# Tying each background sum of a two-layer mixer to the VectorE instruction traced before it

## Chip, cores and metric

One Trainium2 chip, one core of it. The metric is device time in microseconds of one execution of the whole kernel; the profile is one such execution on the same core.

## The reference

The network has two layers, each with one mixer. A mixer normalises 256 latent and 256 context tokens of width 2048, applies a scale and a shift, and projects them with `w_in`. Two attention groups work on the projections (8 heads of grouped-query attention with rotary positions, 8 heads of latent attention), their outputs are gated by a SiLU and projected back by `w_out`, and the result is added to the stream with a gate per channel:

```python
for l in range(DEPTH):
    shift, scale, gate = jnp.split(sc @ w_ada[l] + b_ada[l], 3, axis=-1)
    ...
    h_lat = rms_norm(x, norm_g[l]) * (1.0 + scale[:, None]) + shift[:, None]
    ...
    x = x + gate[:, None] * merge_groups(o_a, lat_a[3], o_b, lat_b[3], w_out[l])
```

What matters here is the first line: `shift`, `scale` and `gate` are matrix-vector products, for two vectors (`c` and `c_ctx`), of 2048 inputs with 6144 outputs in each layer. Everything is float32.

## The kernel before

**The main work.** Each weight matrix is streamed from HBM in tiles of 512 KB. `wtile` (line 107) loads a tile on SP's DMA queue into `raw` (4 buffers), rounds it on ScalarE into `hi` (line 116, 3 buffers) and subtracts it in two halves into `lo` (line 118, 2 buffers). The subtraction runs on VectorE, and on GpSimd (POOL) for every fifth tile. `mm3` (lines 143 to 145) multiplies each pair of tiles three times on TensorE: high by high, low by high, high by low. A tile is reused for 512 tokens in layer 0 and for 256 in most of layer 1. Attention is in `softmax` (lines 605 to 616), `mix` (628, 636) and `attend`; the last VectorE instruction of a head group is the product of line 636 with the gate.

**The background work.** The first layer's shift and scale are made on TensorE at the start. The rest (the first layer's gate, the second layer's scale, shift and gate) is made on VectorE while TensorE multiplies. `ada_rest` (line 308) is a generator that goes through 128 steps. A step (in `ada_half`, line 263) loads 128 rows of the transposed `w_adaT`, 1024 columns at a time, into `rad` (512 KB, 3 buffers), and forms the dot products of these rows with the broadcast vector `cb`: one multiply-and-sum (line 286) for each half row and each of the two vectors, so four VectorE sums a step, and two a step for the second layer's gate, which needs one vector. All sums write their unneeded elementwise product to `junk`, of which there is one buffer. `ada_done` (line 291) adds the two column halves; for scale and shift it writes `mod` (line 208), which the second layer's normalisation reads, and for a gate it transposes the row on TensorE (line 303), copies it (305), stores it to DRAM (306), and `out_steps` loads it again (line 794, `gt`) for the product of line 823 (`go`).

**What sets the order.** The program is traced in one order, and the order of each engine's queue is set from it when the kernel is built, by a modelled timeline (`TCKW`) in which an instruction is queued when its inputs and buffers are there and its priority, its place in the trace, is the best of those that wait. The sums are given a priority 1500 places further back (`BG_LATER`), so they go where nothing else is ready on VectorE. `wtile` traces background steps right after its `lo` instructions, at `bg_rate` steps a tile (1.3, 1.1, 0.5 in layer 0 and 0.4 in layer 1); what is left is traced by `bg_flush` in layer 1, after the first pair of latent heads. `rad` loads are queued on SP behind the last `raw` load (`raw`, line 93), and all loads share SP's queue, in order.

Of the kernel before, what the change touches and what calls it, by code (L numbers as in the profile page):

```python
# [13 lines left out]
ALU = mybir.AluOpType  # L14
# [36 lines left out]
class Net:  # L51
# [211 lines left out]
    def ada_half(self, half, work):  # L263


        nc = self.nc
        hs = slice(half * 1024, half * 1024 + 1024)
        if half not in self.cb:
            self.cb[half] = self.cb_tile()
            with self.behind():  # L270
                nc.sync.dma_start(out=self.cb[half], in_=self.sc_d[:, hs].partition_broadcast(P))
        cb = self.cb[half]
        for l, kind, vs in work:
            if (l, kind) not in self.sums:
                self.sums[l, kind] = [self.cp.tile([P, KT, len(vs)], F32, name=self.nm("as"), tag=f"as{kind}{h}") for h in range(2)]
            out = self.sums[l, kind][half]
            r0 = (0 if l == 0 else D + kind * D)
            for k in range(KT):
                r = self.raw(self.a["w_adaT"][r0 + k * P : r0 + (k + 1) * P, hs], 1, 1024, "rad")[1][:, 0, :]
                for v in vs:  # L280
                    o = out[:, k, v : v + 1]
                    for i in range(NG):
                        cs = slice(i * 1024 // NG, (i + 1) * 1024 // NG)
                        junk = self.tp.tile([P, 1024 // NG], BF16, tag="junk", name=self.nm("junk"), bufs=1)
                        with self.tc.high_priority(offset=-BG_LATER):
                            nc.vector.tensor_tensor_reduce(  # L286
                                out=junk, in0=r[:, cs], in1=cb[:, v, cs], scale=1.0, scalar=o if i else 0.0, op0=ALU.mult, op1=ALU.add, accum_out=o
                            )
                yield

# [924 lines left out]
```

## Time and profile before

| | us |
|---|---|
| median of 3 runs (1394.38 to 1397.32) | 1396.55 |
| the profiled execution | 1398.29 |
| its span, first to last instruction | 1396.5 |
| TensorE (PE) busy | 1328.5 |
| VectorE (DVE) busy | 1078.8 |
| ScalarE (ACT) busy | 580.6 |
| GpSimd (POOL) busy | 404.2 |

The profiled execution lies 1.8 us around its span (what comes before the first and after the last instruction) and 1.7 us above the median. Busy times are sums over the whole span; the stages below have different limits. An engine's instruction shows with its start, its length and, in brackets, how long the engine stood idle before it and what ended that idle time.

### The profile page before, as it was taken

The numbers are of one execution on the slowest core, as the hardware profiler recorded it, in microseconds if no ns is written. First come the engines' busy times: TensorE is split into PE (matmuls) and PEld (weight loads), VectorE is DVE, ScalarE is ACT, GpSimd is POOL, SyncE is SP. The second block draws the span as 40 slices with busy tenths as digits, with TensorE's granted clock in tenths as the row PEclk, the third lists the DMA queues.
The fourth block names the chain that finished last, engine by engine and source line by source line (L and its number), as shares of the span: only waits on it lengthen the run. The fifth ranks groups of instructions, "written<-read, shape, count | busy, mean of one in ns | idle before, by whom it ended". The sixth has DMA issues, their size and how long they took to land.

```text
span 1396.5 us, 21018 instructions
## 1 busy us (share of the span) xinstructions
PE 1328.5 (95%) x7516; PEld 1126.5 (81%) x7516; DVE 1078.8 (77%) x2297; ACT 580.6 (42%) x961; POOL 404.2 (29%) x385
## 2 busy tenths in 40 slices
PE   5999998997999999999999999999999999999996
PEld 5776677786887998788887888889898889888884
DVE  3776589999998999999985536966788676766566
ACT  4322213434351332454532224654554544454543
POOL 0110014533230422222222214433344231323235
PEclk9999999998999999999999999999999999999998
DMA  9997854554635676544465446565866657634444
GB/s 306 331 316 267 307 166 136 166 165 145 185 125 197 217 241 199 167 136 143 170 222 183 149 131 201 175 193 161 268 219 191 195 152 249 234 108 127 159 142 144
DMA packets 141128, 268.31 MB, mean 192 GB/s; under 512 B 8304, under 2 KB 53856, under 8 KB 139616
## 3 DMA queue, kind: packets, MB, share of 16 engines
q1 hardware_dynamic: 141024, 266.97, 59.2%
q8 instruction: 59, 0.97, 0.3%
q14 instruction: 45, 0.37, 0.1%
HBM read 260.61 MB, written 6.33 MB: 191 GB/s over the span
## 4 chain that ended last, share of the span: by engine, by line
PE 50%; DVE 15%; DMA 7%; issue 4%; ACT 3%; POOL 2%; SPq 0%; DVEq 0%; POOLq 0%; ACTq 0%
PE acc L145 14%; PE acc L144 14%; PE acc L143 14%; DVE junk L286 5%; DMA rad<-in_w_adaT 5%; DVE lo L118 4%; PE att L605 3%; DMA raw<-in_w_in 2%; PE att L628 2%; DVE sm L610 1%; PE att L145 1%; PE att L143 1%; PE att L144 1%; DVE y L150 1%; ACT hi L116 1%
## 5 line engine op out<-in xcount | busy, mean ns | idle before, releaser
L116 ACT CAST hi<-raw 128x1024 fp32r<-128x1024 f32 (+2 forms) x279 | 272.0, 977 | 409.4 <-PE acc L144 235.9
L118 DVE TENSOR_TENSOR lo<-raw,hi 128x512 fp32r<-128x512 f32 (+2 forms) x446 | 307.0, 730 | 105.0 <-PE acc L145 47.5
L118 POOL TENSOR_TENSOR lo<-raw,hi 128x512 fp32r<-128x512 f32 (+2 forms) x112 | 153.9, 1395 | 460.5 <-PE acc L145 290.1
L143 PE MATMUL acc<-hi,h 128*128 128x512 f32 (+1 forms) x672 | 239.2, 360 | 7.5 <-DVE g L466 3.8
L144 PE MATMUL acc<-hi,h 128*128 128x512 f32 (+1 forms) x672 | 238.9, 358 | 0.0
L145 PE MATMUL acc<-lo,h 128*128 128x512 f32 (+1 forms) x672 | 227.8, 361 | 6.5 <-DVE lo L118 5.2
L286 DVE CUSTOM_DVE_ANT_0 junk<-rad,cb 128x512 bf16<-128x512 f32 x224 | 167.8, 749 | 67.3 <-DMA rad<-in_w_adaT 65.0
L286 DVE CUSTOM_DVE_ANT_0 junk<-rad,cb,as 128x512 bf16<-128x512 f32 x224 | 190.7, 851 | 3.4
L144 PE MATMUL acc<-h,lo 128*128 128x512 f32 (+1 forms) x512 | 171.0, 340 | 2.7 <-DVE lo L118 2.7
L145 PE MATMUL acc<-h,hi 128*128 128x512 f32 (+1 forms) x512 | 169.9, 338 | 0.0
L616 POOL TENSOR_SCALAR p<-p,sm 128x512 f32<-128x512 f32 (+1 forms) x96 | 86.6, 908 | 277.1 <-DVE sm L614 245.2
L143 PE MATMUL acc<-h,hi 128*128 128x512 f32 (+1 forms) x512 | 163.9, 341 | 1.5 <-DVE g L470 1.2
L143 PEld LDWEIGHTS acc<-hi,h 128*128 128x128 f32 x672 | 127.0, 189 | 30.4 <-issue 8.7
L144 PE MATMUL acc<-hi,y 128*128 128x512 f32 x384 | 149.4, 391 | 0.6 <-DVE y L150 0.6
L143 PE MATMUL acc<-hi,y 128*128 128x512 f32 x384 | 148.8, 393 | 0.8 <-ACT y L149 0.8
L145 PEld LDWEIGHTS acc<-lo,h 128*128 128x128 f32 x672 | 125.1, 190 | 27.6 <-DVE lo L118 8.2
L145 PE MATMUL acc<-lo,y 128*128 128x512 f32 x384 | 143.0, 394 | 2.5 <-DVE lo L118 1.4
L144 PEld LDWEIGHTS acc<-hi,h 128*128 128x128 f32 x672 | 127.3, 190 | 16.1
L144 PEld LDWEIGHTS acc<-h,lo 128*128 128x128 f32 x512 | 96.6, 189 | 13.4 <-DVE lo L118 4.0
L143 PEld LDWEIGHTS acc<-h,hi 128*128 128x128 f32 x512 | 93.4, 189 | 14.2 <-issue 2.5
L145 PEld LDWEIGHTS acc<-h,hi 128*128 128x128 f32 x512 | 96.6, 189 | 9.8
L145 PEld LDWEIGHTS acc<-lo,y 128*128 128x128 f32 x384 | 71.9, 188 | 19.6 <-DVE lo L118 4.2
(218 smaller groups left out, 2254.0 us busy)
## 6 DMA issues: line engine op xcount, KB each, us to landing
rad<-in_w_adaT SPq DMA_DIRECT2D x128, 512.0 KB, 4.6
raw<-in_w_in SPq DMA_DIRECT2D x125, 512.0 KB, 4.4
raw<-in_w_out SPq DMA_DIRECT2D x72, 512.0 KB, 4.1
ra<-in_w_ada SPq DMA_DIRECT2D x32, 1024.0 KB, 9.1
raw<-in_w_in SPq DMA_DIRECT2D x48, 288.0 KB, 3.1
raw<-in_w_ukv SPq DMA_DIRECT2D x16, 512.0 KB, 3.4
raw<-in_w_uq SPq DMA_DIRECT2D x12, 512.0 KB, 3.8
xT<-in_xT SPq DMA_DIRECT2D x8, 512.0 KB, 8.1
```

Of the source, the lines that this page charges most:

```text
L116: nc.scalar.copy(h, t)
L118: e.tensor_tensor(out=lo[:, c], in0=t[:, c], in1=fr(h[:, c]), op=ALU.subtract)
L143: mm(out, lhsT=ah, rhs=bh, start=first, stop=False)
L144: mm(out, lhsT=al, rhs=bh, start=False, stop=False)
L145: return mm(out, lhsT=ah, rhs=bl, start=False, stop=last)
L150: self.nc.vector.tensor_tensor(out=lo, in0=src, in1=fr(hi), op=ALU.subtract)
L286: nc.vector.tensor_tensor_reduce(out=junk, in0=r[:, cs], in1=cb[:, v, cs], scale=1.0, scalar=o if i else 0.0, op0=ALU.mult, op1=ALU.add, a ...
L605: self.order = nc.tensor.matmul(banks[j], lhsT=q[:, qs], rhs=k[:, ks], start=i == 0, stop=i == len(score) - 1)
L610: nc.vector.tensor_reduce(out=nb[:, c], in_=v, axis=AX.X, op=ALU.max)
L616: nc.gpsimd.tensor_scalar(out=pr[j], in0=pr[j], scalar1=l[:, j : j + 1], scalar2=1.0, op0=ALU.mult, op1=ALU.mult)
L628: nc.tensor.transpose(b[:, k, j * P : (j + 1) * P], pr[j][:, (i + k) * P : (i + k + 1) * P], self.ident)
```

## The change

The call that makes a sum is wrapped in one that queues the instruction behind the VectorE instruction traced just before it. It is an order on VectorE's queue alone: the sum may come any distance behind that instruction, and no longer ahead of it. For the first sum of a step the instruction before it is in most cases the second half of the `lo` of the tile that `wtile` has just made; where that `lo` is on POOL, it is whatever VectorE instruction was traced last; within a step it is the sum before.

```diff
                         with self.tc.high_priority(offset=-BG_LATER):
-                            nc.vector.tensor_tensor_reduce(
-                                out=junk, in0=r[:, cs], in1=cb[:, v, cs], scale=1.0, scalar=o if i else 0.0, op0=ALU.mult, op1=ALU.add, accum_out=o
+                            self.tc.keep_in_program_order(
+                                nc.vector.tensor_tensor_reduce(
+                                    out=junk, in0=r[:, cs], in1=cb[:, v, cs], scale=1.0, scalar=o if i else 0.0, op0=ALU.mult, op1=ALU.add, accum_out=o
+                                )
                             )
```

## Rows read from the trace of the kernel before

**Rows 1.** The page's head and busy times: us, share of the span, instructions.

```profile
span 1396.5 us, 21018 instructions
...
PE 1328.5 (95%) x7516; PEld 1126.5 (81%) x7516; DVE 1078.8 (77%) x2297; ACT 580.6 (42%) x961; POOL 404.2 (29%) x385
```

**Rows 2.** Stages: window, length, PE, PEld, DVE, ACT, POOL busy, PEclk, DMA, GB/s.

```profile
174.00:245.00 71.00, 66.44 (x286) 53.77 (x285) 65.39 (x140) 18.40 (x27) 22.14 (x22) 0.98 0.47 149
...
316.00:339.00 23.00, 15.36 (x76) 13.32 (x76) 20.74 (x58) 8.76 (x21) 10.02 (x14) 0.70 0.41 129
...
424.00:476.00 52.00, 47.28 (x255) 40.54 (x254) 44.81 (x104) 12.82 (x25) 16.89 (x16) 0.97 0.58 199
476.00:700.00 224.00, 219.12 (x1299) 193.53 (x1298) 218.00 (x537) 97.70 (x182) 52.77 (x54) 1.00 0.55 178
700.00:772.00 72.00, 71.18 (x345) 58.99 (x344) 50.25 (x117) 23.48 (x40) 17.47 (x15) 1.00 0.57 197
772.00:840.00 68.00, 68.00 (x302) 56.31 (x301) 26.71 (x48) 19.07 (x28) 17.15 (x13) 1.00 0.48 151
...
840.00:868.00 28.00, 28.00 (x127) 23.15 (x126) 17.63 (x22) 12.82 (x17) 12.19 (x12) 1.00 0.65 215
...
985.00:1225.00 240.00, 229.89 (x1496) 207.26 (x1495) 179.05 (x355) 118.44 (x172) 79.65 (x70) 0.99 0.66 213
```

**Rows 3.** Line 286, the sums: ns min/median/max; VectorE idle before them (us, times).

```profile
L286 DVE CUSTOM_DVE_ANT_0 junk<-rad,cb x224: 661/691/1794, 174.5 to 1213.3; 128x512 bf16<-128x512 f32 x112
...
  DMA rad<-in_w_adaT: 65.0, 30
```

**Rows 4.** VectorE's timeline, 433 to 444 us: start, length, instruction, idle before.

```profile
433.61 1.29 DVE L118 TENSOR_TENSOR lo<-raw,hi 128x512 fp32r<-128x512 f32 x2
...
439.69 0.69 DVE L286 CUSTOM_DVE_ANT_0 junk<-rad,cb 128x512 bf16<-128x512 f32 x1 [2.59 <-DMA rad<-in_w_adaT]
...
440.31 3.43 DVE L118 TENSOR_TENSOR lo<-raw,hi 128x512 fp32r<-128x512 f32 x2
```

**Rows 5.** POOL's timeline, 432 to 446 us.

```profile
439.76 3.44 POOL L118 TENSOR_TENSOR lo<-raw,hi 128x512 fp32r<-128x512 f32 x2 [22.78 <-PE acc L145]
```

**Rows 6.** PE's waits, 174 to 245 us: total, times, longest.

```profile
PE acc L143 <- DVE g L466: 3.2, 2, 2.3
PE acc L143 <- DVE kv L466: 1.3, 1, 1.3
```

**Rows 7.** PE's waits, 424 to 476 us.

```profile
PE acc L145 <- DVE lo L118: 4.2, 4, 2.0
```

**Rows 8.** VectorE's waits, 985 to 1225 us.

```profile
DVE junk L286 <- DMA rad<-in_w_adaT: 34.1, 17, 4.1
```

**Rows 9.** VectorE time of line 286 alone, two stages of layer 0.

```profile
245.00:316.00 71.00, 38.37 (x91) 1.00 0.54 170
316.00:339.00 23.00, 10.31 (x30) 0.70 0.41 129
```

**Rows 10.** VectorE's timeline: last instructions of three head groups, and the gate's product.

```profile
338.56 0.42 DVE L636 TENSOR_TENSOR g<-att,g 128x256 f32<-128x256 f32 x1
...
423.88 0.41 DVE L636 TENSOR_TENSOR g<-att,g 128x256 f32<-128x256 f32 x1
...
1255.14 0.42 DVE L636 TENSOR_TENSOR g<-att,g 128x256 f32<-128x256 f32 x1
...
1259.33 1.29 DVE L823 TENSOR_TENSOR go<-acc,gt 128x512 f32<-128x512 f32 x2 [2.72 <-DMA gt<-gate_d]
```

**Rows 11.** VectorE's timeline: the second layer's modulation is written.

```profile
772.71 0.19 DVE L208 TENSOR_TENSOR mod<-as,vec 128x32 f32<-128x32 f32 x1
```

**Rows 12.** ScalarE's timeline: the modulation is first read.

```profile
871.81 1.02 ACT L390 ACTIVATE f<-att,mod,mod 128x256 f32<-128x256 f32 x2 [0.56 <-DVE f L388]
```

**Rows 13.** VectorE's timeline: the last sum of the whole background.

```profile
1215.84 0.75 DVE L286 CUSTOM_DVE_ANT_0 junk<-rad,cb,as 128x512 bf16<-128x512 f32 x1
```

**Rows 14.** SP's waits over the whole span, for a buffer that a sum frees.

```profile
SPq L98 <- DVE as L286: 139.0, 58, 6.8
```

## The prediction

> **What bounds the kernel now.** The page first: PE is busy 1328.5 of 1396.5 us and VectorE 1078.8 [rows 1], so PE is the bound and its holes are all that this change can win. The table of stages says where they are [rows 2]: 4.6 us of idle PE from 174 to 245 (71 less 66.44), 7.6 from 316 to 339, 4.7 from 424 to 476, 4.9 from 476 to 700, 10.1 from 985 to 1225. Beside them stands the granted clock: 0.98, 0.70, 0.97, 1.00 and 0.99. A clock of 0.70 over 23 us has passed 16.1 us of full-speed clock, 6.9 less than the stage is long; in the same way 1.4, 1.6 and 2.4 us are missing in the other stages under 1. PE had stood idle before each of these dips, so a hole there may cost more than its length. Idle and clock together: 6.0 us in the first stage (A), 14.5 in the second (B), 6.3 in the third (C), 12.5 in the last (D), 39.3 in all.
>
> Next, what the holes wait for. From 174 to 245 PE waits 4.5 us for VectorE to empty accumulators [rows 6], from 424 to 476 4.2 us for `lo` [rows 7]. And what holds VectorE up: it stood idle for 65.0 us, 30 times, with a background sum at its head whose `rad` rows had not landed [rows 3], 34.1 us of it in D [rows 8]. The timeline shows the pattern: 2.59 us of waiting, one sum, and only then the pair of `lo` [rows 4], while PE waits for just that. The modelled timeline took the rows as landed earlier than they were.
>
> **The change, part by part.** It adds and removes no instruction, no DMA and no buffer: it costs nothing by itself, and there is no cover to lose. It only moves sums later in VectorE's queue. I laid the 2297 VectorE records [rows 1] beside the kernel's trace order, one by one (no single view shows this): of the 128 steps, 99 begin right after an instruction that is not a sum, 90 of these after a `lo`; 61 of the 99 now run ahead of the instruction that they will be tied to, the other 38 are behind it already, by up to 46 us. The 61 lie in A and C, in stretches around B, from 700 to 820 and in all of D. Those in D run 3 to 16 us ahead of their `lo`, so they move later by as much. The 38 lie from 245 to 330 and from 486 to 700; there the change binds nothing.
>
> What moving wins: a tied sum comes behind its `lo`, which itself needs a `raw` load that SP issued before the `rad` load. So the rows have landed, and the 65.0 us of waiting should nearly go. Only what PE feels of it counts.
> - A: the evacuations behind the sums. Of 6.0 us I take 4, nearly the 4.5 that the waits name.
> - B: two steps, eight sums, some 6 us of VectorE between 316 and 329, will be held until 423.88 (below). The sums that precede B's first hole stay. They are 6 of the stage's 23 us, a quarter, so of 14.5 I take 4.
> - C: the waits for `lo`, 4.2 us [rows 7], behind the waits for `rad` [rows 4]. Of 6.3 I take 4.
> - D: the waits for `rad` stand in front of `lo` and of the attention's small steps. But POOL's and ScalarE's part of the chain stays. Between 0, if PE doesn't feel these waits, and 12.5 I take 7, a little over half, since 17 waits of 2 us on average stand behind 10.1 us of holes.
>
> That is 19 us; the bounds are 0 (the holes have another cause; a loss is the second rival's) and 39.3 (all of them go).
>
> At C the rows say something else too. The `lo` pair took 3.43 us where another took 1.29 [rows 4], and POOL ran its own `lo` pair from 439.76 to 443.20 [rows 5], nearly the same stretch. Without the wait of 2.59 us VectorE's pair starts at 437.1 and is done before POOL's begins, so I count both parts in C's 4. The Trainium skill ("SBUF — State Buffer", section "Who interferes with whom") has it that a VectorE instruction with two SBUF inputs and a GpSimd instruction that reads SBUF shut each other out for a whole instruction; the rows agree. It speaks against the change: sums also have two SBUF inputs, so one moved back may meet POOL's pair instead. By that rule C would give 2 instead of 4, and the sum of the gains would be 17.
>
> What it costs. **First, held steps.** Where a step's tile has its `lo` on POOL, the sum is tied to the last instruction of a head group: the first at 338.56 (by the matching it ran at 220.0), the second at 423.88 (316.3), a third at 1255.14 [rows 10]. Meanwhile each keeps one of three `rad` buffers, and the other steps go through the remaining two. With the tied steps of A and C some 15 us behind, I expect 20 to 30 us of sums to move from before 476 to after 700: from 476 to 700 VectorE is full (218.00 of 224). The idle VectorE time there is 21.8, 41.3 and 10.4 us in the three stages to 868 [rows 2], 73.5 in all. That hides it, and the modulation, written at 772.71 and first read at 871.81, has 99 us to spare [rows 11, 12]. But sums that now come later into a full stretch can lengthen other waits from 476 to 700: between 0 (more sums in a full stretch shorten nothing) and 8 us, nearly twice the 4.9 idle there now; I take 4. If that cover is gone, what comes late next is the second layer's normalisation.
>
> **Second, the last gate.** The last three steps ran by 1215.84 [rows 13]; tied to 1255.14 they need 6 sums of about 0.8 us, so end near 1260.3, and the row must still be transposed, stored, loaded. From 1255.14 to the product at 1259.33 the trace already shows the load alone taking to the end, with VectorE idle 2.72 us for it. I put the product near 1269, 10 us later. It keeps two accumulator banks so much longer. PE has other matmuls, so between 0 and 10 us; I take 3, nearer the hidden end, as the present wait of 2.72 us left PE no hole that the stage table shows.
>
> **Third, SP.** `rad` loads wait for buffers that sums free, 139.0 us in 58 waits, 6.8 the longest [rows 14], and `raw` loads queue behind them in SP. Sums that come later free them later. PE has no hole for a load now, and `raw` is four tiles ahead; I take 0, with 0 to 5 as bounds: not one longest wait more in full.
>
> Sum: 19 less 4, 3 and 0 leaves 12 us. The profiled execution took 1398.29, its span plus 1.8; that gives 1386.3. The median is 1.7 lower: 1384.5, and I say 1384.
>
> **The rivals.** A measurement of this kernel can tell about 0.2%, 2.8 us, from no change.
> - *The stalls only change places.* For it: VectorE is full from 316 to 339 and from 476 to 700, so a sum taken from one hole goes into another, and 38 of 99 ties bind nothing, so that there the change doesn't do what it says. Against it: D has 61 us of idle VectorE in 240, and its rows are waited for, not crowded out. The gains of A and B go back in 476 to 700, D's 7 against the gate's delay: 1396, no change.
> - *Held steps hold everything (slower).* There is one `junk` buffer. If a later sum can't pass a held one, no sum runs from about 229 to 338.9. That defers the 38.4 and 10.3 us of sums there [rows 9]; the second tie and the first gate's transposition could defer 20 more. About 70 us then stand against 73.5 of idle VectorE. It decides when the deferral passes those 73.5: the modulation then comes after 871.81 and PE stands still. At 15 us of such a wait, and some 4 of slower clock after it (B's holes of 7.6 had 6.9), less 12 of gains, it is 1403. For it: the sums now run in trace order without exception. Against it: only data and buffers bind sums of different steps, and a sum that isn't ready need not claim `junk`.
> - *All of D and C goes.* With 12.5 and 6.3 won in full, 4 each in A and B, and 3 given back: 24 us, 1373. The wait names in D include POOL and ScalarE, which speaks against.
>
> **How the numbers follow.** Forecast 0.52; stalls change places 0.20; held steps 0.17; all of D and C 0.11. The forecast's own range is 1377 to 1392: 19 us won with the costs at 0 to the gains at 12 with 8 given back. Of the rival of no change I count 0.03 as faster and 0.03 as slower; of the forecast 0.02 falls short of 2.8 us; of the held steps 0.01 still gives no change. Faster: 0.50 and 0.11 and 0.03, 0.64. Same: 0.14 and 0.02 and 0.01, 0.17. Slower: 0.16 and 0.03, 0.19. The range holds the time 8 times in 10 if it goes from 1369, a little past the third rival, to 1402, which leaves out most of the held steps' case.
>
> **What would show it.** Right: VectorE's idle time for `rad` falls from 65.0 us to under 15; D's PE idle from 10.1 to about 4; the wait for `lo` from 424 to 476 gone; sums gone from 220 to 240 and more of them from 700 to 850; the last sum near 1260 and the product of line 823 near 1269. Wrong: no sums at all from 230 to 338; the modulation written after 860; a hole of several us in PE at 1262 to 1275; longer waits of PE from 476 to 700.

## The result and the profile after

The changed kernel takes 1383.26 us (median of 4 runs, 1375.19 to 1385.2) against 1395.53 us (4 runs, 1394.38 to 1397.32): ratio 0.9895, 95% interval 0.987 to 0.9919. The forecast was 1384.0, counted from the median of 1396.55 known then: a gain of 12.5 us, against 12.3 measured. The profiled execution took 1385.2 us. Lines from 287 on have moved by one or two: the sums are line 287, the last product of a head group 638, the gated product 825.

The page of the changed kernel, head and busy times, against [rows 1]: the engines do the same work, in a span 13.1 us shorter.

```profile
span 1383.4 us, 21025 instructions
...
PE 1322.7 (96%) x7516; PEld 1125.6 (81%) x7516; DVE 1084.3 (78%) x2297; ACT 581.3 (42%) x961; POOL 398.1 (29%) x385
```

Line 287 in the changed kernel, with what VectorE's idle time before it waited for, against [rows 3]: 65.0 us of waiting for `rad` have become 0.6.

```profile
L287 DVE CUSTOM_DVE_ANT_0 junk<-rad,cb x224: 661/691/1790, 197.5 to 1246.3; 128x512 bf16<-128x512 f32 x112
...
  DMA rad<-in_w_adaT: 0.6, 1
```

The stages of the changed kernel, columns as in [rows 2]:

```profile
174.00:245.00 71.00, 68.92 (x307) 56.61 (x307) 58.22 (x118) 20.48 (x28) 24.32 (x23) 1.00 0.42 126
...
316.00:339.00 23.00, 20.38 (x110) 17.29 (x111) 18.47 (x46) 14.38 (x25) 9.26 (x14) 0.93 0.24 87
...
424.00:476.00 52.00, 48.95 (x315) 46.06 (x314) 46.64 (x115) 14.00 (x27) 18.74 (x18) 0.97 0.62 185
476.00:700.00 224.00, 216.75 (x1238) 188.54 (x1237) 217.82 (x522) 99.58 (x184) 56.02 (x54) 0.99 0.54 175
700.00:772.00 72.00, 67.97 (x313) 55.29 (x312) 67.38 (x157) 19.33 (x32) 18.11 (x13) 0.95 0.69 235
772.00:840.00 68.00, 65.40 (x282) 53.62 (x281) 60.69 (x133) 18.33 (x27) 18.26 (x13) 0.97 0.64 210
...
985.00:1225.00 240.00, 236.59 (x1567) 215.75 (x1566) 177.31 (x362) 127.25 (x191) 79.05 (x72) 1.00 0.66 217
```

A and B lost most of their holes, D two thirds of its idle time (10.1 to 3.4 us). But from 700 to 840 there are new holes: 0.8 us of idle PE before, 6.6 now, and clocks of 0.95 and 0.97, which pass 5.6 us less of full-speed clock in 140.

Where the gain stands along the way is read from instructions that both kernels have. VectorE's timeline of the changed kernel at the last instructions of head groups, against [rows 10], and ScalarE's first reads of the modulation (count, ns, first and last start), against [rows 12]:

```profile
326.19 0.42 DVE L638 TENSOR_TENSOR g<-att,g 128x256 f32<-128x256 f32 x1 [0.51 <-PE att L145]
...
408.28 0.42 DVE L638 TENSOR_TENSOR g<-att,g 128x256 f32<-128x256 f32 x1 [2.37 <-PE att L145]
...
1241.34 0.41 DVE L638 TENSOR_TENSOR g<-att,g 128x256 f32<-128x256 f32 x1
```

```profile
L392 ACT ACTIVATE f<-att,mod,mod x10: 553/562/573, 871.7 to 899.3; 128x256 f32<-128x256 f32 x10
```

The first layer's gated products, before and then after (14 each, first and last start):

```profile
L823 DVE TENSOR_TENSOR go<-acc,gt x14: 675/688/693, 746.0 to 861.0; 128x512 f32<-128x512 f32 x14
```

```profile
L825 DVE TENSOR_TENSOR go<-acc,gt x14: 674/680/692, 734.2 to 860.9; 128x512 f32<-128x512 f32 x14
```

The lead of the changed kernel is 12.4 us at the first of these head groups (338.56 less 326.19), 15.6 at the second, 11.8 at the first gated product, **0.1 at the last one** and at the second layer's start (871.81 and 871.7), then 13.8 at the third head group and 13.1 at the end. In these two executions the first layer gave back all that it won, and the second layer won the whole result (other executions keep 1 to 5 us, below).

What was given back, and how: TensorE's waits from 700 to 772 and from 772 to 840 in the changed kernel (us in total, times, longest), then VectorE's timeline before the first of them:

```profile
PE acc L145 <- DVE lo L118: 3.7, 2, 3.4
...
PE acc L145 <- DVE lo L118: 2.6, 1, 2.6
```

```profile
748.26 0.69 DVE L287 CUSTOM_DVE_ANT_0 junk<-rad,cb 128x512 bf16<-128x512 f32 x1
...
748.99 1.63 DVE L287 CUSTOM_DVE_ANT_0 junk<-rad,cb,as 128x512 bf16<-128x512 f32 x1
...
750.55 2.34 DVE L118 TENSOR_TENSOR lo<-raw,hi 128x512 fp32r<-128x512 f32 x2
```

and POOL's at the same time:

```profile
748.58 3.16 POOL L118 TENSOR_TENSOR lo<-raw,hi 128x512 fp32r<-128x512 f32 x2 [1.81 <-ACT hi L116]
```

Sums stand in VectorE's queue ahead of the `lo` that TensorE needs, and the sum beside POOL's pair takes 1.63 us and the `lo` pair 2.34, against 0.69 (0.75 for this second sum of a row) and 1.29 elsewhere [rows 4]. That is the price which the Trainium skill ("SBUF — State Buffer", "Who interferes with whom") let one expect of a sum moved back; here it fell near 750, not in C. By these figures it is some 2 us (0.9 on the sum, 1.05 on the pair) of the wait of 3.4. Near 800 the `lo` pair takes 1.29 us with POOL idle beside it, and TensorE still waits 2.6: there it is mostly the sums ahead of it.

Why so many sums were still there is the first sums' view, line 287 from 262 to 327 us in the changed kernel (count, ns, first and last start):

```profile
L287 DVE CUSTOM_DVE_ANT_0 junk<-rad,cb,as x2: 1786/1820/1855, 262.7 to 267.7; 128x512 bf16<-128x512 f32 x2
L287 DVE CUSTOM_DVE_ANT_0 junk<-rad,cb x2: 682/922/1162, 265.0 to 326.5; 128x512 bf16<-128x512 f32 x2
```

After the sum at 267.7 none starts until 326.54, just behind the head group's last product at 326.19. VectorE's time on sums by stage, in the changed kernel, says what was put off: 8.81 us from 245 to 316, against 38.37 [rows 9], and 89.7 us from 700 to 840.

```profile
245.00:316.00 71.00, 8.81 (x16) 0.98 0.37 110
316.00:339.00 23.00, 6.13 (x16) 0.93 0.24 87
...
700.00:772.00 72.00, 46.44 (x115) 0.95 0.69 235
772.00:840.00 68.00, 43.29 (x104) 0.97 0.64 210
```

### The profile page after: what moved, and what is told of

It is laid out like the page before. It is cut to its first block, busy times and chain, and to the rows that moved or that the text cites. A ratio compares the mean times of both kernels' runs of the same rounds, so it can differ in the third digit from the quotient of the medians.

```text
span 1383.4 us, 21025 instructions
## 1 busy us (share of the span) xinstructions
PE 1322.7 (96%) x7516; PEld 1125.6 (81%) x7516; DVE 1084.3 (78%) x2297; ACT 581.3 (42%) x961; POOL 398.1 (29%) x385
## 4 chain that ended last, share of the span: by engine, by line
PE 73%; DVE 15%; DMA 4%; issue 3%; POOL 2%; ACT 1%; SPq 1%; DVEq 0%; POOLq 0%; ACTq 0%
PE acc L143 20%; PE acc L145 20%; PE acc L144 20%; DVE junk L287 6%; PE att L607 4%; DVE lo L118 3%; PE att L630 2%; DMA ra<-in_w_ada 2%; PE att L240 2%; PE att L145 1%; PE att L144 1%; PE att L143 1%; DMA raw<-in_w_in 1%; DVE sm L612 1%; DMA y<-y_d 1%
## 5 line engine op out<-in xcount | busy, mean ns | idle before, releaser
L118 POOL TENSOR_TENSOR lo<-raw,hi 128x512 fp32r<-128x512 f32 (+2 forms) x112 | 149.0, 1350 | 441.2 <-PE acc L145 253.0
L145 PE MATMUL acc<-lo,h 128*128 128x512 f32 (+1 forms) x672 | 225.0, 358 | 2.5 <-POOL lo L118 1.3
L287 DVE CUSTOM_DVE_ANT_0 junk<-rad,cb,as 128x512 bf16<-128x512 f32 x224 | 187.2, 836 | 3.6
L287 DVE CUSTOM_DVE_ANT_0 junk<-rad,cb 128x512 bf16<-128x512 f32 x224 | 175.5, 783 | 3.6 <-DMA rad<-in_w_adaT 0.6
L618 POOL TENSOR_SCALAR p<-p,sm 128x512 f32<-128x512 f32 (+1 forms) x96 | 81.3, 852 | 305.0 <-DVE sm L616 282.0
L145 PE MATMUL acc<-lo,y 128*128 128x512 f32 x384 | 146.0, 400 | 8.7 <-DVE lo L118 7.7
L144 PE MATMUL acc<-hi,y 128*128 128x512 f32 x384 | 151.8, 397 | 0.7 <-DVE y L150 0.6
L143 PE MATMUL acc<-hi,y 128*128 128x512 f32 x384 | 150.1, 397 | 1.1 <-ACT y L149 0.9
L144 PEld LDWEIGHTS acc<-h,lo 128*128 128x128 f32 x512 | 97.3, 190 | 11.8 <-DVE lo L118 2.3
L143 PEld LDWEIGHTS acc<-h,hi 128*128 128x128 f32 x512 | 94.1, 190 | 12.4 <-issue 2.1
```

The lines of the kernel that those rows point to most:

```text
L118: e.tensor_tensor(out=lo[:, c], in0=t[:, c], in1=fr(h[:, c]), op=ALU.subtract)
L143: mm(out, lhsT=ah, rhs=bh, start=first, stop=False)
L144: mm(out, lhsT=al, rhs=bh, start=False, stop=False)
L145: return mm(out, lhsT=ah, rhs=bl, start=False, stop=last)
L287: nc.vector.tensor_tensor_reduce(out=junk, in0=r[:, cs], in1=cb[:, v, cs], scale=1.0, scalar=o if i else 0.0, op0=ALU.mult, op1=ALU.add, a ...
L618: nc.gpsimd.tensor_scalar(out=pr[j], in0=pr[j], scalar1=l[:, j : j + 1], scalar2=1.0, op0=ALU.mult, op1=ALU.mult)
```

## The experiments

All kernels were timed against the kernel before on the same chip. "Second layer" is the first read of its modulation, in the profiled execution, as in [rows 12].

| kernel | median us | ratio to before, 95% | second layer from |
|---|---|---|---|
| changed kernel | 1383.26 | 0.9895 (0.987 to 0.9919) | 871.7 |
| tie in layer 1 alone | 1385.33 | 0.9922 (0.9911 to 0.9934) | 871.0 |
| tie in layer 0 alone | 1392.45 | 0.9977 (0.9964 to 0.9989) | 870.4 |
| behind a `lo` only | 1377.77 | 0.9869 (0.9856 to 0.9881) | 866.0 |
| sums at lower priority | 1381.37 | 0.9893 (0.9881 to 0.9906) | 867.1 |
| held steps with own product buffer | 1398.0 | 1.0019 (1.0006 to 1.0032) | 881.0 |
| behind a `lo`, step 9 held | 1379.06 | 0.988 (0.9858 to 0.9901) | 868.1 |
| behind a `lo`, step 12 held | 1378.47 | 0.9867 (0.9843 to 0.9891) | 861.8 |
| behind a `lo`, step 15 held | 1375.17 | 0.9836 (0.9809 to 0.9863) | 862.8 |
| behind a `lo`, step 18 held | 1376.97 | 0.9849 (0.9827 to 0.9871) | 862.7 |
| layer 1 behind a `lo` | 1380.72 | 0.9894 (0.9874 to 0.9914) | 867.3 |

**Each layer alone.** The first layer's steps make sums for two vectors; only the last 32 steps, for the second layer's gate, make them for one. The diff ties those alone; the other kernel has `== 2`.

```diff
+if len(vs) == 1:
     self.tc.keep_in_program_order(s)
```

> Only the 32 steps of the second layer's gate are tied (they run from 985 us on); layer 0's sums stay as before. Theory: behind their lo these sums no longer wait for rad rows, PE's idle time from 985 to 1225 falls from 10.1 to about 3.4 us and its clock stays up, about 9 us in all: 1386.5. Rival (the gain is that the first attention runs without sums; in layer 1 stalls only change places): within 2 us of before, 1394 to 1397.

> Only the steps with two vectors are tied (all of layer 0's); the second layer's gate stays free. Theory: A wins 4, B 10, C 2, and the sums that come late give 12 to 14 back between 476 and 840: about 1392, and from 985 on the waits for rad rows are as before (34 us of VectorE). Rival (the gain is layer 0's): 1383 to 1386.

Measured: 1385.33 and 1392.45 us, 10.2 and 3.1 us under the kernel before (1395.54 beside them). They add up to 13.3, against 12.3 for both at once, which is the same within the intervals: nothing here shows the two parts touching each other. Both times are near their theories' (1386.5 and about 1392), and layer 0 alone comes near the first rival's "stalls only change places". The stage 985 to 1225 with the tie in layer 1 alone is that of the changed kernel; with the tie in layer 0 alone VectorE waits there for `rad` as in [rows 8].

```profile
985.00:1225.00 240.00, 236.76 (x1571) 216.08 (x1570) 177.67 (x363) 128.59 (x192) 79.35 (x73) 1.00 0.67 216
```

```profile
DVE junk L286 <- DMA rad<-in_w_adaT: 32.4, 17, 4.0
```

**Ties to a `lo` only.** Every sum is queued behind the last `lo` that VectorE made, so no step is held by a head group's end.

```diff
+z = e.tensor_tensor(out=lo[:, c], in0=t[:, c], in1=fr(h[:, c]), op=ALU.subtract)
+self.lo_dve = z if e is nc.vector else self.lo_dve
...
+with self.tc.issue_after(self.lo_dve.ins):
     nc.vector.tensor_tensor_reduce(
```

> Each sum is tied to the last lo that VectorE was given, never to the end of a head group, so no step is held for long. Theory: the waits for rad rows go as in the changed kernel, the sums keep nearly their old rate in layer 0, so the stalls at 752 and 801 us don't come, and the second layer's last gate is ready early; A, C and D win 15, B nothing: about 1380. Rival (holding the sums off the first attention is what wins): B's holes come back in full, 1388 or more.

Measured: 1377.77 us, and its interval just overlaps the changed kernel's. The stages 316 to 339 and 700 to 772 of this kernel show both sides of the hold: B's hole is back, as the rival had it, and the later one is gone, with 34.5 us of sums in the second stage instead of 46.4. The total is not the rival's 1388: what the changed kernel's hold wins in B it loses again later.

```profile
316.00:339.00 23.00, 17.53 (x83) 15.06 (x83) 20.94 (x55) 8.42 (x19) 10.21 (x14) 0.70 0.34 108
...
476.00:700.00 224.00, 216.81 (x1262) 189.47 (x1261) 218.70 (x529) 97.69 (x180) 56.77 (x54) 1.00 0.55 176
700.00:772.00 72.00, 71.57 (x347) 59.59 (x347) 56.71 (x127) 22.78 (x39) 18.60 (x15) 1.00 0.65 221
```

**Sums at lower priority.** `BG_LATER` 4000 instead of 1500, to let a late `lo` pass the sums.

> The changed kernel with the sums' priority 4000 places back and not 1500. In the changed kernel the sums lag up to 170 us, about 1500 places of the trace, from 570 to 760 us. Theory: by then their priority is no longer behind that of the main work, which is why sums stand ahead of lo at 752 and 801 us; with 4000 these stalls go, about 8 us: 1375, and the modulation is still written before 871. Rival (GpSimd's use of the memory port and full VectorE make the stalls, not priority): 1383; if the sums starve and the modulation comes late, above 1390.

Measured: 1381.37 us, with both stalls as they were. The order of every engine's queue came out as in the changed kernel, so this says nothing of priority as a remedy; it is a second sample of the changed kernel.

**Who is held by a held step.** Six held steps of layer 0 get a product buffer of their own.

```diff
-junk = self.tp.tile([P, 1024 // NG], BF16, tag="junk", name=self.nm("junk"), bufs=1)
+held = self.nst in (7, 8, 20, 21, 32, 33)
+junk = self.tp.tile([P, 1024 // NG], BF16, tag="junkh" if held else "junk", name=self.nm("junk"), bufs=1)
```

> The kernel after, but the six steps of layer 0 that are queued behind the end of an attention group or behind the gate row's copy (steps 7, 8, 20, 21, 32 and 33) write their unused product into a buffer of their own. Theory: in the kernel after, a held step keeps every later sum back because all sums write one product buffer, which is handed out in trace order. With its own buffer the other sums pass it: VectorE's time on sums from 245 to 316 us goes up from 8.7 to 25 us or more, the stage 316 to 339 gives back part of its gain (TensorE busy 20.4 down to about 18.5 us), fewer sums are left for 700 to 840 (88.9 down to about 75 us), and the total stays within 4 us of the kernel after, 1379 to 1385 us. Rival: it is the three w_adaT buffers (or the order of the accumulators) that hold the others; then the sums from 245 to 316 stay near 9 us and the stages stay as in the kernel after, 1381 to 1385 us.

Measured: the mechanism is as the theory says, the time is not. With the extra buffer the other sums pass: VectorE's time on sums from 245 to 316 goes from 8.81 to 23.04 us and in 700 to 840 from 89.7 to 71.1. So it was the one product buffer, given out in trace order, that made a held step hold all. But the kernel takes 1398.0 us, 13 more than the top of what either side expected. Its stage B is as bad as before the change, the stall near 750 is there too (TensorE busy 67.44 of 72 us from 700 to 772, with 43.6 us of sums), and VectorE's waits for `rad` are back, 30.2 us; the timeline shows one in the middle of the attention, with the probabilities' `pt` pair queued behind it:

```profile
316.00:339.00 23.00, 15.31 (x79) 12.25 (x80) 19.57 (x50) 7.69 (x16) 10.22 (x14) 0.78 0.27 84
```

```profile
  DMA rad<-in_w_adaT: 30.2, 18
```

```profile
315.11 0.69 DVE L290 CUSTOM_DVE_ANT_0 junk<-rad,cb 128x512 bf16<-128x512 f32 x1 [2.70 <-DMA rad<-in_w_adaT]
...
315.73 1.28 DVE L151 TENSOR_TENSOR pt<-att,pt 128x512 fp32r<-128x512 f32 x2
```

**One hold, and where.** Ties to a `lo` only, but step N is queued behind the last product of the first attention, so that it and the later steps stay out of the rest of it.

```diff
-with self.tc.issue_after(self.lo_dve.ins):
+with self.tc.issue_after((self.head if self.nst == N else self.lo_dve).ins):
...
+self.head = nc.vector.tensor_tensor(out=yo, in0=o, in1=yo, op=ALU.mult)
```

> Every sum queued behind the last low part that is on VectorE, and step 9 alone queued behind the last VectorE product of the first attention, so that steps 9 and later are out of that attention and no other step is held. Theory: the gain of the kernel after in 316 to 339 us (TensorE busy 20.4 of 23 us, granted clock 0.93, against 17.5 us at 0.70 with every sum behind a low part) can be had without the stalls at 752 and 801 us, since only one hold delays the sums: TensorE over 137 of 140 us from 700 to 840 and the total 1370 to 1375 us. Rival: what is put off comes back as stalls later whatever holds it: 700 to 840 falls to 134 us as in the kernel after, total 1377 to 1382 us.

> As the run with step 9 held, but step 12 is the one held, so 12 more sums are done before the first attention ends and 12 fewer are put off. Theory: about the same gain in 316 to 339 us, less to catch up: 1370 to 1375 us, within 2 us of the run with step 9. Rival: the sums that run before 316 us still delay that attention, so the stage stays near 17.5 us busy at 0.70 to 0.8 and the total is 1376 to 1379 us.

> As the run with step 12 held, but step 15 is the one held: 60 sums ahead of the last product of the first attention instead of 48, 12 fewer put off. Theory: the stall near 750 us comes from the backlog of sums that stand ahead of a low part on VectorE (46 to 47 us of sums from 700 to 772 where TensorE waits 3.6 us, 34.5 us where it does not wait), so a smaller backlog ends it while the first attention still runs free: TensorE over 70.5 of 72 us from 700 to 772, over 20 of 23 us from 316 to 339, and the total 1371 to 1375 us. Rival: sums in the first attention are back before the backlog is small enough, so one of the two stages stays slow: 1376 to 1380 us.

> Step 18 is the one held, 72 sums ahead of that product, against 79 with no step held. Theory: the backlog is nearly that of the kernel with no step held, so no stall near 750 us, but the sums run into the first attention: TensorE near 18 of 23 us from 316 to 339, total 1376 to 1379 us. Rival: any hold frees the last part of that attention: over 20 of 23 us, total 1371 to 1375 us.

Measured: 1379.06, 1378.47, 1375.17, 1376.97 us. The first two are within the rivals' ranges, and neither beats ties to a `lo` only; with step 12 it is only the time that the rival has right, for its cause, a slow stage 316 to 339, did not come (20.44 us at a clock of 1.00). Step 15 lands at the upper edge of its theory's range (1371 to 1375) and has the lowest median here, though the intervals of all four overlap. Step 18 is within its theory's range. The stages 316 to 339, 700 to 772 and 772 to 840, with step 9, 15 and 18 held:

```profile
316.00:339.00 23.00, 20.64 (x111) 17.62 (x110) 18.86 (x46) 13.54 (x24) 8.97 (x14) 0.93 0.23 82
...
700.00:772.00 72.00, 67.77 (x306) 54.72 (x305) 67.27 (x154) 19.86 (x33) 17.18 (x13) 0.95 0.71 233
772.00:840.00 68.00, 65.65 (x281) 53.54 (x280) 43.27 (x86) 19.63 (x30) 20.37 (x14) 0.97 0.51 166
```

```profile
316.00:339.00 23.00, 21.56 (x117) 17.41 (x118) 20.18 (x49) 15.10 (x27) 9.14 (x15) 1.00 0.22 81
...
700.00:772.00 72.00, 67.31 (x320) 54.88 (x319) 62.83 (x139) 20.38 (x33) 17.21 (x13) 1.00 0.66 220
772.00:840.00 68.00, 68.00 (x302) 56.33 (x301) 31.11 (x59) 20.90 (x31) 18.71 (x14) 1.00 0.49 155
```

```profile
316.00:339.00 23.00, 19.78 (x109) 16.15 (x108) 19.89 (x49) 11.68 (x21) 8.23 (x14) 0.91 0.34 125
...
700.00:772.00 72.00, 71.82 (x344) 59.54 (x343) 56.40 (x126) 21.58 (x34) 16.84 (x13) 1.00 0.65 217
```

The later the hold, the less is put off, and the stalls leave one by one: with step 9 held there are both, with 12 and 15 only the one near 750 (40.6 us of sums from 700 to 772 with step 15), with 18 neither (34.9 us). In the other direction B fills up again: 20.64, 21.56, 19.78 and, with no hold, 17.53 us of TensorE. Step 15 was expected to be free of the stall near 750 and was not; counted in sums from 700 to 772, the backlog that ends it lies between 34.9 and 40.6 us. Sums that run before 316 us do the stage B no harm: with step 12 held 22.9 us of them lie in 245 to 316, as many as with own product buffers (23.0), and B keeps 20.44 us of TensorE.

**The last gate.** Layer 0 as changed, layer 1 behind a `lo`, so that the last three steps don't wait for the head group at 1241.

> Layer 0 as in the kernel after; in layer 1 each sum is queued behind the last low part on VectorE, so that the last three steps no longer wait for the last product of the attention group near 1241 us. Forecast's term: the late last gate costs 3 us, so the total falls by 3 us, to 1378 to 1380 us, and the first gated product comes earlier after the last matmul before it. Rival: the late gate costs nothing since TensorE has other work (no hole from 1245 to 1275 us in the kernel after): 1381 to 1384 us, and the difference of some 5 us between the kernel after and the one with all sums behind a low part lies wholly in layer 0.

Measured: 1380.72 us, ratio 0.9894, against 0.9895 and 0.9893 for the two samples of the changed kernel. The time lies between the two ranges, and the medians can't tell 3 us from nothing: each interval reaches some 2 us or more to either side. The traces can. The head groups' products before and behind the late sums, in the kernel before, the changed kernel and this one:

```profile
1247.88 0.42 DVE L636 TENSOR_TENSOR g<-att,g 128x256 f32<-128x256 f32 x1 [0.55 <-PE att L145]
...
1351.73 0.42 DVE L636 TENSOR_TENSOR g<-att,g 128x256 f32<-128x256 f32 x1 [0.82 <-PE att L145]
```

```profile
1233.55 0.42 DVE L638 TENSOR_TENSOR g<-att,g 128x256 f32<-128x256 f32 x1 [0.55 <-PE att L145]
...
1338.38 0.42 DVE L638 TENSOR_TENSOR g<-att,g 128x256 f32<-128x256 f32 x1
```

```profile
1228.34 0.42 DVE L641 TENSOR_TENSOR g<-att,g 128x256 f32<-128x256 f32 x1 [0.55 <-PE att L147]
...
1332.21 0.42 DVE L641 TENSOR_TENSOR g<-att,g 128x256 f32<-128x256 f32 x1 [0.82 <-PE att L147]
```

The lead over the kernel before falls from 14.33 to 13.35 us in the changed kernel and stays at 19.5 in this one. In all four kernels whose last sums wait for that head group (the changed one, layer 1 alone, lower priority, own product buffer) it falls by 0.95 to 0.98 us, and in the seven others by no more than 0.02. The late gate, with its late sums, costs 1.0 us.

## Why the prediction was right, and where it was not

The total is right to 1 us, and that is in good part luck: the gains came out some 10 us higher than the 19 forecast, a cost that was put at nothing came to 11.7, and the two cancel. What held is the way in which the change wins, sums that no longer wait for `rad` in front of the main work. By the leads above:

- **A, 4 us: right.** A `lo` that VectorE began at 300.17 us in the kernel before begins at 295.81, 4.4 us earlier, and the stage's idle and clock time falls from 6.0 to 2.1 us.
- **B, 4 us: too low.** The lead grows from there to 12.4 at the end of the first attention, so B gave 8; by the stage's idle and clock time, 14.5 before and 4.2 now, it gave 10. The step that failed is "The sums that precede B's first hole stay": they were held too, and no sum runs in the stage until that attention's last product at 326.19.
- **C, 4 us: near, 2.8.** The 15.6 us of lead at 408.28 are VectorE's alone: that product moved ahead in its queue, while ScalarE's rounding of a tile at 410.60 is 12.5 ahead. ScalarE's rounding of a tile behind C, in the kernel before and in the changed one, is 15.2 ahead, so C's code gave 2.8. The wait for `lo` is gone, but TensorE now waits 3.1 us for POOL's normalisation from 424 to 476, with a clock of 0.97.

```profile
495.00 0.68 ACT L116 CAST hi<-raw 128x576 fp32r<-128x576 f32 x1 [2.40 <-DVE as L286]
```

```profile
479.82 0.67 ACT L116 CAST hi<-raw 128x576 fp32r<-128x576 f32 x1 [2.21 <-issue]
```

- **476 to 700, 4 us of loss: right in size, its cause not shown.** The lead falls from 15.2 to 11.8 at the first gated product. But sums take less of VectorE there than before (115.1 us, against 121.1), and with ties to a `lo` only, where no step is held, TensorE is busy 216.81 us of this stage, against 216.75. So it is not shown that late sums cause it.
- **Deferred sums hidden in idle VectorE time, 0: wrong, by 11.7 us.** This is the step that failed: "Meanwhile each keeps one of three `rad` buffers, and the other steps go through the remaining two." The second rival's premise held instead: one product buffer, and a held step holds everything. Nearly 60 us more of sums than before (89.7 against 30.2 from 700 to 840, in the kernel before 23.3 and 6.9) then met the `lo` that TensorE waits for. Idle VectorE time summed over a stage did not hide them: what counts is what stands ahead of one `lo` in one queue. The rival's own price, 15 us because the modulation comes after its reader, did not occur; it was written by 822.4, 49 us early.
- **D, 7 us: too low.** From 0.1 of lead at 871.7 to 14.3 at 1233.55 is 14.2; with the tie in layer 1 alone the medians give 10.2. The waits for `rad` were the cause of most of D's 12.5 us, as the third rival had it for this stage; 3.4 of idle TensorE are left.
- **The last gate, 3 us of loss: right in its course, its price 1.0.** The last sum starts at 1247.07 and the product of line 825 at 1257.94, 1.4 us ahead of the kernel before where the third head group is 13.8 ahead, so 12 us late, where 10 were forecast, and it waits for its load; but TensorE had other work for most of that, and the lead falls by 1.0 us (shown above).
- **SP, 0: right.** Waits for buffers that sums free went from 139.0 us in 58 [rows 14] to 160.8 in 76, with no hole from it.

The terms so measured: 4.4 + 8 + 2.8 - 3.4 - 11.7 + 14.2 - 1.0 - 0.2 at the end = 13.1, the difference of the spans. They are differences of leads, so they must add up; where one ends and the next begins is a choice of instruction. The forecast assumed that other sums pass the held steps. The run that comes nearest to that is the one with own product buffers: there they pass, the rows that they use are not there in time, and it takes 1398.0 us. So the forecast's own course would not have led to its number. The signs that were named came out (`rad` waits 0.6, D's idle 3.4, no wait for `lo` from 424 to 476, more sums after 700), and so did two named as signs against: no sum starts between 267.7 and 326.5, and TensorE's idle time from 476 to 700 grew from 4.9 to 7.3 us.

What the first layer keeps differs from execution to execution; what it gives back hardly does. In three other kernels VectorE's order is that of the changed kernel up to 822 us: tie in layer 0 alone, lower priority, layer 1 behind a `lo`. Their gated products of the first layer, in this order:

```profile
L825 DVE TENSOR_TENSOR go<-acc,gt x14: 675/680/692, 734.4 to 859.6; 128x512 f32<-128x512 f32 x14
...
L825 DVE TENSOR_TENSOR go<-acc,gt x14: 675/680/691, 730.7 to 856.3; 128x512 f32<-128x512 f32 x14
...
L828 DVE TENSOR_TENSOR go<-acc,gt x14: 675/680/692, 729.2 to 856.5; 128x512 f32<-128x512 f32 x14
```

Against the kernel before, their lead falls from 11.6 to 1.4, from 15.3 to 4.7 and from 16.8 to 4.5 us, and the changed kernel's from 11.8 to 0.1: each gives back 10.2 to 12.3 us, with stalls near 750 and 800. So the 11.7 are usual; it is the gain won before, 11.6 to 16.8 us, that varies. From 316 to 339 the granted clock was 0.93 in the two with the smaller gain and 1.00 in the two with the larger, which is 1.6 us of it; the rest was not settled. By the medians the first layer's tie is worth 3.1 us.

## What to carry to other kernels

A queue order that ties filler work to the instruction traced before it is right where that instruction is the one whose input was loaded first, and a hidden hold where it is anything else; tie to the named producer. A single scratch buffer, given out in trace order, turns the hold of one piece into the hold of all; but a second buffer is no remedy by itself, if the pieces let past then wait for their own inputs (1398.0 us here). Work that is put off must be placed by what stands ahead of a critical instruction at its due time, not by idle time summed over a stage; one deliberate hold, set by trying four places, came out best (1375.17 us, against 1383.26 with the held steps as traced; its lead over 1377.77 with none is within the intervals, and so is that over the other three places).

## What had not been expected of the hardware

Much the same hole near 750 us was followed by different granted clocks: over 700 to 772 it was 0.95 in the changed kernel, with layer 1 behind a `lo` and with step 9 held, 0.98 in the changed kernel's second sample and 1.00 with steps 12 and 15 held, where TensorE had waited as long (3.2 to 3.5 us the longest in all of them). A mean of 0.95 is a part of the stage at the lower of the clock's two levels, 1.2 GHz, and the rest at 2.4. Between 0.95 and 1.00 lie 3.6 us of full-speed clock in this stage. It may be part of why step 12's times fall into two groups (1373.75 and 1373.92, then 1378.47 to 1381.09); no run here separates the two. The changed kernel's four executions spread over 10 us in the same way: 1385.2, 1384.85, 1381.68 and 1375.19 us came with a granted clock of 0.987, 0.988, 0.989 and 0.995 over the whole execution.
